# A decoder layer's first stage with its input scaling on ScalarE and low weight parts on VectorE, and its first query operands made during the value projections

## The chip, the cores and the metric

The kernel runs on one core of one Trainium2 chip. A core has five engines that run side by side, each from a queue of its own: TensorE (PE, with its weight loads, PEld), VectorE (DVE), ScalarE (ACT), GpSimd (POOL) and SyncE (SP), which here issues the DMAs. The metric is the device time of one execution in microseconds (us), the median of the runs shown.

## The reference

One layer for 1024 tokens of width 1024. What touches the change:

```python
mod = silu(c) @ w_mod + b_mod            # shift1, scale1, gate1, shift2, scale2, gate2
h   = x * (1.0 + scale1) + shift1
q, k, v, u, iq, ik, iw = split(h @ w_in) # 8 heads of 64; iq: 8 index heads of 64, ik: one
# rope on q, k, iq, ik
score = sum_h iw_h * relu(iq_h . ik)     # causal, one row per token
idx   = top_k(score, 256)                # per token
s = q . k / 8, only for keys in idx; softmax; o = p @ v
x = layer_norm(ALPHA * x + gate1 * (concat(o, pooled u) @ w_o))
x = layer_norm(ALPHA * x + gate2 * swiglu(x * (1 + scale2) + shift2))
```

## The kernel before

The 1024 tokens are eight tiles of 128. Matrices are kept as pairs of parts, a high part and a low part (the rest that rounding leaves), and a product is three passes of matmuls (high x high, high x low, low x high). `split(dst, raw, n, lo_eng)` makes such a pair of a weight block: the high part is a copy on ACT, the low part a subtraction on `lo_eng`, by default DVE (V). All instructions go through small queue objects, so each stands at one helper line (L174, DMAs L168) in the profile, and is told by its names.

Stages, with their times in the profiled execution:

1. **First stage, to 65 us.** Loop over the eight blocks j of 128 input channels (`for j in range(KT)`, L331): two dot products on DVE give scale and shift of the block (`mj`, in `const_C`); ACT makes hT's high part from the input `xt`; DVE scales `xt` in place (L350) and subtracts to get hT's low part; every second j the weights `WS[j // 2]` (`ws_W`) of the index query are split (L353), with the low part on DVE for j = 0 and on POOL for j = 2, 4, 6. Matmuls then add block j to the index queries of tiles 2 to 6 (`iq`) and to the index key (`ik`).
2. **Ropes and operands, to 87 us.** DVE ropes the index query of tile 2 and the index key (`ikt`, `ikr`); the weights of q (wq, four blocks into the same `ws_W`) are split at L457 to L463, low parts of blocks 0 and 2 on POOL, of 1 and 3 on DVE; POOL ropes tiles 3 to 7 (`iqraw`, `ptmp`); then the operands of the index scores (`ikE`, `ikO`, `qa`, `ql`). Projections `pj` fill PE in between.
3. **Index scores (lg), 87 to about 175 us**, tile by tile, with the q projections as filler. From then on the search for the 256 largest scores of each row runs as "streams": `bisect()` is a generator that yields before each piece of work with its engine and its length, and goes over bits of a 15-bit key, first of the high half of the score and then of the low half. There are four streams: tile 3, and tiles 5 and 4, whose rounds run on ACT (`keysA`, `junkB`, `colsA`); tile 2 (`LATE`; `keysA`, `colsE`, 128x384) and tiles 7 and 6 (`keysD`), whose rounds run on DVE. A planner models each queue's time; whenever an instruction would leave its engine idle for long enough, `fill()` puts the next piece of a stream ahead of it (`advance()`). LATE is not filled while tile 7 is being searched. `need(i)` runs the stream of tile i to its end at once.
4. **Projections, to 349 us**: 24 groups (`n_` = 0 to 23), eight of u, eight of k, eight of v, with `at_(n, f)` to put work behind group n. Then the operands of the queries of tiles 7 and 6 are made: `q_load` (DMA), `q_transpose` (PE, `qT`), `q_operands` (four ACT copies and two DVE subtractions each, `qab`).
5. **Attention, 365 to about 500 us**: 32 units of a tile and a head pair. A unit is `u_scores` (PE, `s`), masking by the searched scores with a row maximum on DVE (`sm_H`, `stat_X`), exponentials on ACT, transposes (`pT`) and the product with v (`pair`, `o`). Scores run two units ahead (`AHEAD`). Tiles 7 and 6 come first, then 5 and 4, 3 and 2, 1 and 0.
6. **Output projection, normalisation and the gated FFN (gu, dn), to 1291 us.**

While `pinned` holds an engine's letter, its instructions stay in the order in which the planner wrote them; elsewhere the scheduler may move them.

Of the kernel before, what the change touches and what calls it, by code (L numbers as in the profile page):

```python
# [186 lines left out]
def decoder_layer_kernel(  # L187
# [143 lines left out]
    for j in range(KT):  # L331
        wm = wmr[j % 3]
        for hf in range(2):
            SP.dma_start(wm[:, hf * 1024 : (hf + 1) * 1024], wma_in[j][:, hf * 1024 : (hf + 1) * 1024])
        xt = xtr[j % 7]
        SP.dma_start(xt, xT_in[j])
        if j == 0:
            SP.dma_start(bcol, bcol_in)
        if j % 2 == 0:
            raw_iq = raw_slot()  # L340
            SP.dma_start(raw_iq, wiq_in[j // 2])
        if j == 0:
            SP.dma_start(wik_raw, wikw_in)
        mj = m1[:, 2 * j : 2 * j + 2]
        for hf in range(2):
            dot(wm[:, hf * 1024 : (hf + 1) * 1024], mj[:, hf : hf + 1])
        V.tensor_tensor(mj, mj, bcol[:, 2 * j : 2 * j + 2], ALU.add)
        V.tensor_scalar(mj[:, 0:1], mj[:, 0:1], 1.0, None, ALU.add)
        A.activation(hT[j][:, 0:1024], xt, AF.Identity, bias=mj[:, 1:2], scale=mj[:, 0:1])
        V.tensor_scalar(xt, xt, mj[:, 0:1], mj[:, 1:2], ALU.mult, ALU.add)  # L350
        V.tensor_tensor(hT[j][:, 1024:2048], xt, f_(hT[j][:, 0:1024]), ALU.subtract)
        if j % 2 == 0:
            split(WS[j // 2], raw_iq, 1024, G if j else V)  # L353
        if j == 0:
            split(wik, wik_raw, 576)
        for t in range(2, 7):
            mm_k(psq[t], lambda k, a: hh(k, a, t * P, P), lambda k, b: ww(k, b, 0, 512), [j])
        for c in range(2):
            mm_k(psk[c][0:72, :], lambda k, b: wikk(k, b), lambda k, a: hh(k, a, c * 512, 512), [j])
# [95 lines left out]
                        float(np.float32(8.0 ** -0.5)), None, ALU.mult)  # L455
    rope_tok(V, iq_raw(2), iqtmp, 2)
    for kp in range(3):  # L457
        split(WS[kp], raws[kp], 1024, V if kp == 1 else G)
    raws[3] = raw_slot()
    SP.dma_start(raws[3], wq_in[3])  # L460
    for i in range(3, 7):
# [96 lines left out]
    biased = set()  # L558

    def bisect(tiles, cols, on_act):  # L560

# [9 lines left out]
        one = lambda c, m: c[:, m : m + 1]  # L571
        w_ = lambda i: (i + 1) / 8
        for m, i in enumerate(tiles):
            yield "V", 1.13 * w_(i)
            V.tensor_scalar(trash(i), score(i), 0.0, 0.0, ALU.is_ge, ALU.add, accum_out=one(cntc, m))
        yield "V", 0.6
        V.tensor_scalar(pr, cntc, float(TOPK), None, ALU.is_ge)
        V.tensor_scalar(sg, pr, 2.0, -1.0, ALU.mult, ALU.add)
        V.tensor_scalar(flip, pr, 32768.0, -32768.0, ALU.mult, ALU.add)
# [10 lines left out]
        sum_w = sum(w_(i) for i in tiles)  # L590

        def search_v(bits, base, low):
            V.memset(cand, float(1 << (bits - 1)))
            for b in range(bits - 1, -1, -1):
                yield "V", 0.4 + 1.08 * sum_w + 0.35 * nt
                for m, i in enumerate(tiles):
                    dt = U16 if low else I16
                    V.tensor_scalar(trash(i).bitcast(dt), kv[i].bitcast(dt), one(cand, m), one(base, m),
                                    ALU.is_ge, ALU.add, accum_out=one(cntc, m))
                off = -float(1 << (b - 1)) if b > 0 else -1.0  # L600
                for m in range(nt):
                    V.tensor_scalar(one(pr, m), one(cntc, m), 0.0, float(1 << b), ALU.is_ge, ALU.mult)
                for m in range(nt):
                    V.tensor_scalar(one(cand, m), one(pr, m), one(cand, m), off, ALU.add, ALU.add)

        def search_a(bits, low):

            V.memset(cand, 0.5 - float(1 << (bits - 1)))
            for b in range(bits - 1, -1, -1):
# [367 lines left out]
    qabh = buf("H", 14336, 1536, "qab", F32R)  # L977
    qabw = [buf("W", 2048 * i, 1536, "qab", F32R) for i in (0, 1)]
    qabx = [buf("X", 5312 + i * 1536, 1536, "qab", F32R) for i in (0, 1)]
    qab = {7: qabh, 6: qabw[0], 5: qabw[1], 4: qabw[0], 3: qabh, 2: qabx[0], 1: qabx[1], 0: qabh}  # L980

    qops = {}

    def q_load(i):
        raw = raw_slot()[:, 0:512]
        SP.dma_start(raw, q_d[i])
        return raw

    def q_make(i, raw, pt=None):
        b = qab[i]  # L990
        qops[i] = (b[:, 0:1024], b[:, 1024:1536])
        q_operands(pt if pt is not None else q_transpose(raw), *qops[i])

    for s_ in (last, last + 1):
        if s_ == last:
            qr = {i: q_load(i) for i in (7, 6)}
            qp = {i: q_transpose(qr[i]) for i in (7, 6)}
        for f in late.pop(s_, []):
            f()
    assert not late, late  # L1000
    for i in (7, 6):
        q_make(i, qr[i], qp[i])

    def cat_slot(g):
        return WS[g]

# [870 lines left out]
```

## Time and profile before

| | us |
|---|---|
| median of 3 runs | 1292.34 (1291.21 to 1293.01) |
| profiled execution | 1293.41, of which span 1291.6 |
| PE busy | 1200.3 (93%) |
| DVE busy | 994.8 (77%) |
| POOL busy | 722.5 (56%) |
| ACT busy | 654.5 (51%) |
| granted TensorE clock, mean | 0.972 of full |

The execution's own time is 1.8 us longer than the span of its instructions. A row of the waits reads: engine, its operation, the engine and the operation that it waited for, total time, how often, the longest. A row of instructions reads: start, duration, engine, line, operation, output and inputs, shapes, count; in brackets the idle time ahead of it and what ended that.

### The profile page before, as it was taken

Reading aid. Unit: us, or ns where it says so; the run is one execution under the profiler, and the core shown is the slowest. Engines: PE = TensorE matmul, PEld = TensorE weight load, DVE = VectorE, ACT = ScalarE, POOL = GpSimd, SP = SyncE. Lnnn points to the kernel's source line nnn. Section 1 sums busy time; section 2 is a strip of 40 time slices with the busy share of each in tenths; the row PEclk is TensorE's granted clock in tenths of the full one; section 3 lists DMA queues with packets and bytes.
Section 4 is the critical chain, followed back from the end, with each engine's and each line's share of the span. In section 5 each row is a group of like instructions: output and inputs, shape, how many; then the busy total and the mean of one; then the engine's idle time right before and its main releaser. Section 6 shows DMA issues by size and latency. Waiting matters only on the chain.

```text
span 1291.6 us, 16411 instructions
## 1 busy us (share of the span) xinstructions
PE 1200.3 (93%) x5622; PEld 932.2 (72%) x5622; DVE 994.8 (77%) x1845; ACT 654.5 (51%) x1343; POOL 722.5 (56%) x510
## 2 busy tenths in 40 slices
PE   7979999999879999997799999999999999999996
PEld 6656565687646666886678787878888787878775
DVE  6758998877979866568687778687877777687798
ACT  3346878797668687265443333343433333333531
POOL 1383375657012355267666657483847566576848
PEclk9989999999958999999899999999999999999998
DMA  9510048521000016300111021201121110203112
GB/s 350 200 72 17 10 159 321 196 82 57 17 1 17 9 50 214 129 9 9 65 66 66 33 82 34 82 33 66 33 65 39 60 66 33 90 33 107 49 66 114
DMA packets 32460, 103.40 MB, mean 80 GB/s; under 512 B 3573, under 2 KB 3573, under 8 KB 28793
## 3 DMA queue, kind: packets, MB, share of 16 engines
q1 hardware_dynamic: 32376, 102.36, 22.5%
q8 instruction: 44, 0.72, 0.2%
q14 instruction: 40, 0.32, 0.1%
HBM read 92.90 MB, written 9.45 MB: 79 GB/s over the span
## 4 chain that ended last, share of the span: by engine, by line
PE 60%; DVE 18%; POOL 9%; issue 7%; ACT 5%; DMA 1%; SPq 0%; DVEq 0%; POOLq 0%; ACTq 0%
PE gu L174 24%; PE dn L174 14%; PE pj L174 5%; PE wo L174 4%; PE pair L174 3%; PE s L174 2%; PE pT L174 2%; PE o L174 2%; DVE act_W L174 2%; DVE score_X L174 2%; POOL wraw_R L174 2%; DVE junk_X L174 2%; PE lg L174 2%; DVE utmp_X L174 1%; POOL ws_W L174 1%
## 5 line engine op out<-in xcount | busy, mean ns | idle before, releaser
L174 PE MATMUL gu<-hr_H,wblk_T 128*128 128x512 f32 (+1 forms) x924 | 217.5, 388 | 6.1 <-ACT gtmp_V L174 2.7
L174 PE MATMUL gu<-hr_H,wblk_V 128*128 128x512 f32 (+1 forms) x924 | 215.8, 385 | 4.3 <-POOL wblk_V L174 2.1
L174 PEld LDWEIGHTS gu<-hr_H,wblk_T 128*128 128x128 f32 x924 | 172.2, 191 | 42.4 <-POOL wblk_T L174 3.6
L174 PEld LDWEIGHTS gu<-hr_H,wblk_V 128*128 128x128 f32 x924 | 169.9, 188 | 41.4 <-POOL wblk_V L174 4.2
L174 DVE TENSOR_TENSOR res_X<-res_X,dn 128x512 f32<-128x512 f32 (+1 forms) x253 | 159.0, 679 | 15.4 <-PE dn L174 15.3
L174 PE MATMUL pj<-ws_W,hT_H 128*128 128x512 f32 x456 | 117.3, 406 | 8.8 <-POOL ws_W L174 6.7
L174 POOL TENSOR_TENSOR wraw_R<-wraw_R 128x512 f32<-128x512 f32 x64 | 94.6, 1486 | 47.0 <-DVE wblk_T L174 23.7
L174 POOL TENSOR_TENSOR wraw_W<-wraw_W 128x512 f32<-128x512 f32 x60 | 86.9, 1456 | 59.6 <-DVE wblk_V L174 29.3
L174 POOL TENSOR_SCALAR sm_H<-sm_H,stat_X 128x1024 f32<-128x1024 f32 (+7 forms) x64 | 48.0, 764 | 124.1 <-DVE stat_X L174 96.0
L174 PEld LDWEIGHTS pj<-ws_W,hT_H 128*128 128x128 f32 x456 | 85.0, 192 | 33.2 <-POOL ws_W L174 7.0
L174 PE MATMUL dn<-wblk_T,act_W 128*128 128x512 f32 x324 | 78.8, 391 | 4.3 <-DVE act_W L174 4.3
L174 PE MATMUL dn<-wblk_V,act_W 128*128 128x512 f32 x324 | 78.5, 391 | 2.9 <-DVE act_W L174 2.5
L174 DVE TENSOR_SCALAR_CACHE_REDUCE junk_X<-keysD_T,colsD_X 128x1024 int16<-128x1024 int16 (+1 forms) x64 | 78.9, 1268 | 0.2
L174 ACT ACTIVATE wblk_V<-wraw_R 128x512 fp32r<-128x512 f32 x56 | 35.2, 629 | 81.2 <-POOL wraw_R L174 62.7
L174 POOL TENSOR_TENSOR ws_W<-raw_R,ws_W 128x1024 fp32r<-128x1024 f32 x17 | 44.3, 2625 | 53.4 <-ACT ws_W L174 53.4
L174 PEld LDWEIGHTS dn<-wblk_T,act_W 128*128 128x128 f32 x324 | 60.4, 188 | 18.9 <-DVE act_W L174 6.4
L174 PEld LDWEIGHTS dn<-wblk_V,act_W 128*128 128x128 f32 x324 | 60.4, 188 | 17.4 <-DVE act_W L174 4.2
L174 ACT ACTIVATE wblk_V<-wraw_W 128x512 fp32r<-128x512 f32 x53 | 33.1, 627 | 75.0 <-POOL wraw_W L174 56.4
L174 ACT ACTIVATE wblk_T<-wraw_W 128x512 fp32r<-128x512 f32 x56 | 35.0, 628 | 65.9 <-POOL wraw_W L174 50.2
L174 ACT ACTIVATE wblk_T<-wraw_R 128x512 fp32r<-128x512 f32 x52 | 32.5, 627 | 60.5 <-POOL wraw_R L174 44.5
L174 ACT ACTIVATE utmp_X<-gu 128x512 f32<-128x512 f32 x33 | 19.7, 598 | 74.7 <-PE gu L174 74.7
L174 ACT ACTIVATE sm_H<-sm_H,stat_X 128x1024 f32<-128x1024 f32 (+7 forms) x64 | 49.1, 771 | 16.7 <-DVE stat_X L174 16.5
(295 smaller groups left out, 2763.7 us busy)
## 6 DMA issues: line engine op xcount, KB each, us to landing
mset_K<-in_wmr_dram SPq DMA_DIRECT2D x16, 1024.0 KB, 5.6
wm_K<-in_wma_dram SPq DMA_DIRECT2D x16, 512.0 KB, 10.0
wraw_R<-in_wg_dram SPq DMA_DIRECT2D x6, 1024.0 KB, 4.8
wraw_R<-in_wd_dram SPq DMA_DIRECT2D x12, 512.0 KB, 3.7
wraw_W<-in_wup_dram SPq DMA_DIRECT2D x12, 512.0 KB, 3.7
wraw_R<-in_wup_dram SPq DMA_DIRECT2D x10, 512.0 KB, 3.6
wraw_W<-in_wg_dram SPq DMA_DIRECT2D x5, 1024.0 KB, 4.9
wraw_W<-in_wd_dram SPq DMA_DIRECT2D x10, 512.0 KB, 3.5
```

The costliest lines, as they stand in the source:

```text
L174: ins_ = f(*a, **k)
```

## The change

In the first two stages the in-place scaling of `xt` becomes an ACT activation with the same scale and shift; the low parts of the index query's weights for j = 2, 4, 6 and of wq's blocks 0 and 2 go from POOL to DVE.

```diff
         A.activation(hT[j][:, 0:1024], xt, AF.Identity, bias=mj[:, 1:2], scale=mj[:, 0:1])
-        V.tensor_scalar(xt, xt, mj[:, 0:1], mj[:, 1:2], ALU.mult, ALU.add)
+        A.activation(xt, xt, AF.Identity, bias=mj[:, 1:2], scale=mj[:, 0:1])
         V.tensor_tensor(hT[j][:, 1024:2048], xt, f_(hT[j][:, 0:1024]), ALU.subtract)
         if j % 2 == 0:
-            split(WS[j // 2], raw_iq, 1024, G if j else V)
+            split(WS[j // 2], raw_iq, 1024)
         if j == 0:
             split(wik, wik_raw, 576)
...
     for kp in range(3):
-        split(WS[kp], raws[kp], 1024, V if kp == 1 else G)
+        split(WS[kp], raws[kp], 1024)
 
```

The rest is about the queries and searches. The operands of tiles 7 and 6 are made at groups 20 and 21, in buffers of their own (`qabv`, in V), from loads written at group 17; before, they are made behind the last group. From the last group on until the first two units are written, `hold` keeps `fill()` from placing any stream but the one of tiles 7 and 6 on DVE. DVE searches yield per tile and no longer per round of all their tiles. With every yield comes a flag that decides between streams that could start at the same time, and the pinning of a stream's first piece, which was LATE's alone, is given to every open stream behind the first two units.

```diff
             for b in range(bits - 1, -1, -1):
-                yield "V", 0.4 + 1.08 * sum_w + 0.35 * nt
                 for m, i in enumerate(tiles):
+                    yield "V", 0.3 + 1.08 * w_(i) + (0.35 * nt if m == nt - 1 else 0.0)
...
-        held = st[3] == LATE and st[4] and "V" not in pinned
+        held = st[4] and q.name not in pinned
...
-            todo = [st for st in streams if not (first and st[3] == LATE) and st[1][0] == q.name and start(st) + st[1][1] <= until + SLACK.get(q.name, 0.0)]
+            todo = [st for st in streams if not (first and st[3] == LATE) and not (hold and (q.name == "A" or 7 not in st[3])) and st[1][0] == q.name and start(st) + st[1][1] <= until + SLACK.get(q.name, 0.0)]
             if not todo:
                 return
-            advance(min(todo, key=lambda st: (start(st), st[3] not in TILES_A)))
+            advance(min(todo, key=lambda st: (start(st), not (len(st[1]) > 2 and st[1][2]))))
...
+    qabv = [buf("V", 4096 + 1536 * i, 1536, "qab", F32R) for i in (0, 1)]
+    qab = {7: qabv[0], 6: qabv[1], 5: qabw[1], 4: qabw[0], 3: qabh, 2: qabx[0], 1: qabx[1], 0: qabh}
...
+        if n_ == len(groups) - 1:
+            hold.append(1)
+        if n_ == 17:
+            qr.update((i, q_load(i)) for i in (7, 6))
+        if n_ in (20, 21):
+            at_(n_, lambda i=27 - n_: q_make(i, qr[i]))
...
     for s_ in (last, last + 1):
-        if s_ == last:
-            qr = {i: q_load(i) for i in (7, 6)}
-            qp = {i: q_transpose(qr[i]) for i in (7, 6)}
         for f in late.pop(s_, []):
             f()
     assert not late, late
-    for i in (7, 6):
-        q_make(i, qr[i], qp[i])
-
...
         u_exp(u)
+    hold.clear()
+    for st in streams:
+        st[4] = True
     u_norm(units[0])
```

What the engines' sequences of instructions show of it, at three places. A row is line, operation, output and inputs with their buffer numbers, and the output's shape.

POOL behind its constants, the first stage and the ropes, before (`ws_W` are low weight parts, `ptmp_C` and `iqraw_V` the ropes):

```order
L174 TENSOR_TENSOR ws_W_70<-raw_R_74,ws_W_70 128x1024
L174 TENSOR_TENSOR ws_W_71<-raw_R_75,ws_W_71 128x1024
L174 TENSOR_TENSOR ws_W_72<-raw_R_73,ws_W_72 128x1024
L174 TENSOR_TENSOR ws_W_69<-raw_R_74,ws_W_69 128x1024
L174 TENSOR_TENSOR ptmp_C_455<-iqraw_V_447,gr_G_76 128x512
```

and, behind three ropes and the first piece of the fourth, the last low part of wq among them:

```order
L174 TENSOR_TENSOR iqraw_V_447<-iqraw_V_447,ptmp_C_455 128x512
L174 TENSOR_TENSOR ptmp_C_455<-iqraw_V_447,gr_G_76 128x512
L174 TENSOR_TENSOR ws_W_71<-raw_R_73,ws_W_71 128x1024
L174 TENSOR_TENSOR iqraw_V_447<-iqraw_V_447,gr_G_76 128x512
L174 TENSOR_TENSOR iqraw_V_447<-iqraw_V_447,ptmp_C_455 128x512
```

and now:

```order
L174 MEMSET const_C_78 128x256
L174 AFFINE_SELECT const_C_78<-const_C_78 128x128
L174 TENSOR_TENSOR ptmp_C_455<-iqraw_V_447,gr_G_76 128x512
L174 TENSOR_TENSOR iqraw_V_447<-iqraw_V_447,gr_G_76 128x512
L174 TENSOR_TENSOR iqraw_V_447<-iqraw_V_447,ptmp_C_455 128x512
```

The ropes stand first on POOL now; no low weight part is left among or ahead of them.

DVE from the last block's low part of hT to the operands of the index scores, before (rows of the ropes between the first and the second piece are left out):

```order
L174 TENSOR_TENSOR const_C_78<-const_C_78 128x2
L174 TENSOR_SCALAR const_C_78<-const_C_78 128x1
L174 TENSOR_SCALAR xt_V_94<-xt_V_94,const_C_78 128x1024
L174 TENSOR_TENSOR hT_H_68<-xt_V_94,hT_H_68 128x1024
L174 TENSOR_TENSOR iqtmp_V_448<-iqraw_V_447,gr_G_76 128x512
```

```order
L174 TENSOR_SCALAR const_C_78<-ikt_477 128x32
L174 TENSOR_TENSOR ikr_X_499<-ikr_X_499,ikt_X_500 128x256
L174 TENSOR_TENSOR ws_W_70<-raw_R_75,ws_W_70 128x1024
L174 TENSOR_TENSOR ws_W_72<-raw_R_74,ws_W_72 128x1024
L174 TENSOR_TENSOR ikE_K_554<-ikT_563,ikE_K_554 64x512
```

and now:

```order
L174 TENSOR_TENSOR hT_H_68<-xt_V_94,hT_H_68 128x1024
L174 TENSOR_TENSOR ws_W_69<-raw_R_74,ws_W_69 128x1024
L174 TENSOR_TENSOR ws_W_70<-raw_R_75,ws_W_70 128x1024
L174 TENSOR_TENSOR iqtmp_V_448<-iqraw_V_447,gr_G_76 128x512
L174 TENSOR_TENSOR iqraw_V_447<-iqraw_V_447,gr_G_76 128x512
```

```order
L174 TENSOR_SCALAR const_C_78<-ikt_477 128x32
L174 TENSOR_TENSOR ikr_X_499<-ikr_X_499,ikt_X_500 128x256
L174 TENSOR_TENSOR ws_W_71<-raw_R_73,ws_W_71 128x1024
L174 TENSOR_TENSOR ws_W_72<-raw_R_74,ws_W_72 128x1024
L174 TENSOR_TENSOR ikE_K_554<-ikT_563,ikE_K_554 64x512
```

The scaling of `xt` is gone; two low parts of wq stand ahead of the rope of tile 2, two behind the ropes of the index key as before, so that the operands still follow a pair of low parts.

DVE around the first attention unit (`sm_H` from `s` is its masking, `junk_X` with `keysA_X` 128x384 a round of tile 2, `keys_T` and `junkA_T` the end of the search of tiles 5 and 4), before:

```order
L174 TENSOR_SCALAR colsE_X_610<-colsE_X_610 128x1 x2
L174 TENSOR_SCALAR junk_X_608,colsE_X_610<-keysA_X_599,colsE_X_610 128x384
L174 TENSOR_TENSOR qab_H_2672<-qT_2679,qab_H_2672 64x512 x2
L174 ISA sm_H_2671,stat_X_2666<-s_2757,score_X_77 128x1024
L174 ISA stat_X_2666 128x1
L174 TENSOR_TENSOR qab_W_2673<-qT_2684,qab_W_2673 64x512 x2
L174 ISA sm_H_2671,stat_X_2666<-s_2758,score_X_77 128x1024
```

and now:

```order
L174 TENSOR_SCALAR junkA_T_606,colsA_X_600<-score_X_77,colsA_X_600 128x640
L174 TENSOR_SCALAR colsA_X_600<-colsA_X_600 128x1
L174 TENSOR_SCALAR colsE_X_610<-colsE_X_610 128x1 x4
L174 TENSOR_TENSOR qab_V_1314<-qT_2660,qab_V_1314 64x512 x2
L174 ISA sm_H_2746,stat_X_2741<-s_2752,score_X_77 128x1024
L174 ISA stat_X_2741 128x1
```

and seven rows on:

```order
L174 RECIPROCAL stat_X_2741<-stat_X_2741 128x2
L174 ISA sm_H_2746,stat_X_2741<-s_2787,score_X_77 128x1024
L174 ISA stat_X_2741 128x1
L174 TENSOR_SCALAR score_X_77<-score_X_77 128x640
L174 TENSOR_TENSOR keysA_X_599<-score_X_77,colsE_X_610 128x384
L174 MEMSET colsE_X_610 128x1
L174 TENSOR_TENSOR keys_T_604<-keys_T_604,score_X_77 128x640
L174 TENSOR_SCALAR junk_X_608,colsE_X_610<-keysA_X_599,colsE_X_610 128x384
```

The rounds of tile 2 and the query operands stood ahead of the first masking; now one low part of tile 6 stands there, and the end of tile 4's search and the rounds of tile 2 come behind the maskings of the first two units. On ACT the copies of `qab_V` now stand among the last value copies, where `qab_H` and `qab_W` stood behind them. SP's queue of loads keeps its sequence.

More of the change, by code (lines that the diff above doesn't have):

```diff
@@ L556, in decoder_layer_kernel @@
     keys = {i: kw.bitcast(I16) for i, kw in keys.items()}
-    biased = set()
+    biased, hold = set(), []
     def bisect(tiles, cols, on_act):
@@ L573, in bisect @@
         for m, i in enumerate(tiles):
-            yield "V", 1.13 * w_(i)
+            yield "V", 1.13 * w_(i), on_act
             V.tensor_scalar(trash(i), score(i), 0.0, 0.0, ALU.is_ge, ALU.add, accum_out=one(cntc, m))
-        yield "V", 0.6
+        yield "V", 0.6, on_act
         V.tensor_scalar(pr, cntc, float(TOPK), None, ALU.is_ge)
@@ L583, in bisect @@
         for m, i in enumerate(tiles):
-            yield "V", 1.1 * w_(i)
+            yield "V", 1.1 * w_(i), on_act
             hv = score(i).bitcast(I16).rearrange("p (n two) -> p n two", two=2)
@@ L589, in bisect @@
                 V.tensor_scalar(one(thr, m), one(kp, m), 2.0, float(P * (i + 1) + 1), ALU.mult, ALU.add)
-        sum_w = sum(w_(i) for i in tiles)
         def search_v(bits, base, low):
@@ L619, in search_a @@
                     A.activation(one(cand, m), one(pr, m), AF.Identity, scale=-0.5 * float(1 << b), bias=one(cand, m))
-            yield "V", 0.1
+            yield "V", 0.1, True
             V.tensor_scalar(cand, cand, -1.0, None, ALU.mult)
@@ L625, in bisect @@
         for m, i in enumerate(tiles):
-            yield "V", 1.8 * w_(i)
+            yield "V", 1.8 * w_(i), on_act
             V.tensor_scalar(trash(i).bitcast(I16), kv[i], one(M, m), one(kp, m), ALU.is_gt, ALU.add,
@@ L666, in open_stream @@
         b = bisect(*a)
-        streams.insert(0, [T.t, next(b), b, a[0], True])
+        streams.insert(0, [T.t, next(b), b, a[0], a[0] == LATE])
         times.fill = fill
@@ L675, in advance @@
         q = queues[st[1][0]]
-        held = st[3] == LATE and st[4] and "V" not in pinned
+        held = st[4] and q.name not in pinned
         st[4] = False
         if held:
-            pinned.add("V")
+            pinned.add(q.name)
         try:
@@ L685, in advance @@
         if held:
-            pinned.discard("V")
+            pinned.discard(q.name)
         times.fill = fill
@@ L915, in take, with q_load, q_make @@
         at_(slot, lambda: k_transpose(t, raw))
+    qabh = buf("H", 14336, 1536, "qab", F32R)
+    qabw = [buf("W", 2048 * i, 1536, "qab", F32R) for i in (0, 1)]
+    qabx = [buf("X", 5312 + i * 1536, 1536, "qab", F32R) for i in (0, 1)]
+    qabv = [buf("V", 4096 + 1536 * i, 1536, "qab", F32R) for i in (0, 1)]
+    qab = {7: qabv[0], 6: qabv[1], 5: qabw[1], 4: qabw[0], 3: qabh, 2: qabx[0], 1: qabx[1], 0: qabh}
+    qops = {}
+    def q_load(i):
+        raw = raw_slot()[:, 0:512]
+        SP.dma_start(raw, q_d[i])
+        return raw
+    def q_make(i, raw, pt=None):
+        b = qab[i]
+        qops[i] = (b[:, 0:1024], b[:, 1024:1536])
+        q_operands(pt if pt is not None else q_transpose(raw), *qops[i])
     groups = [("u", g, c) for g in (3, 2, 1, 0) for c in range(2)] + [("k", t, 0) for t in range(NT)] + [("v", t, 0) for t in range(NT)]
@@ L920, in decoder_layer_kernel @@
     held, pair = {}, None
+    qr = {}
     for n_, (kind, a, b) in enumerate(groups):
+        if n_ == len(groups) - 1:
[4 more added lines that the diff above has]
+            at_(n_, lambda i=27 - n_: q_make(i, qr[i]))
         if n_ in PAIRS:
@@ L976, in decoder_layer_kernel @@
     smr = buf("H", 8192, 6144, "sm")
[L977 to L992, printed above, removed]
     for s_ in (last, last + 1):
-        if s_ == last:
-            qr = {i: q_load(i) for i in (7, 6)}
-            qp = {i: q_transpose(qr[i]) for i in (7, 6)}
         for f in late.pop(s_, []):
```

## The prediction

> **What bounds the kernel now.** I read the page's busy rows first, then TensorE's row by slices, then what TensorE waited for where that row dips, then those stretches in windows and instruction by instruction. The sum is made against the profiled execution, 1293.4 us with a span of 1291.6; the median of the three runs, 1292.3, lies 1.1 below it.
>
> ```profile
> PE 1200.3 (93%) x5622; PEld 932.2 (72%) x5622; DVE 994.8 (77%) x1845; ACT 654.5 (51%) x1343; POOL 722.5 (56%) x510
> PE   7979999999879999997799999999999999999996
> PEclk9989999999958999999899999999999999999998
> ```
>
> TensorE (PE) works 93% of the span. A slice is 32.3 us. What the change can reach is in the dips: slices 1 and 3 (up to 97 us), and slices 11 and 12 (323 to 387 us), of which the twelfth ran at about half the TensorE clock; the dips at 581 to 646 and at the end lie outside the change. Elsewhere PE is the limit, and a shorter time of another engine is worth nothing. What PE waited for, first up to 100 us, then from 280 to 520 us (total, times, longest):
>
> ```profile
> PE pj L174 <- POOL ws_W L174: 6.7, 1, 6.7
> PE iq L174 <- POOL ws_W L174: 3.7, 3, 1.4
> PE iq L174 <- DVE hT_H L174: 1.2, 2, 0.6
> ```
>
> ```profile
> PE s L174 <- ACT qab_H L174: 8.8, 1, 8.8
> PE s L174 <- DVE qab_H L174: 3.9, 1, 3.9
> ```
>
> Both edits aim at these rows: the low weight parts of stage one (ws_W) and the first query operands (qab_H). Windows say who is full there (PE, weight load, VectorE (DVE), ScalarE (ACT), POOL busy; then PE clock, DMA share, GB/s):
>
> ```profile
> 16.15:64.70 48.55, 43.63 (x177) 31.87 (x178) 40.32 (x59) 14.75 (x16) 13.94 (x5) 0.96 0.69 269
> 40.00:45.00 5.00, 3.64 (x16) 2.58 (x15) 4.93 (x8) 0.00 (x1) 2.35 (x1) 1.00 1.02 406
> 45.00:50.00 5.00, 5.00 (x23) 3.75 (x23) 4.42 (x8) 1.58 (x2) 0.00 (x0) 1.00 0.32 129
> 82.00:87.00 5.00, 4.86 (x11) 3.80 (x12) 0.00 (x0) 0.00 (x0) 4.76 (x5) 0.50 0.57 210
> 175.00:325.00 150.00, 144.99 (x689) 103.16 (x688) 122.72 (x298) 120.43 (x311) 96.57 (x60) 0.99 0.43 159
> 325.00:349.00 24.00, 24.00 (x112) 19.88 (x111) 23.84 (x57) 13.75 (x38) 0.00 (x0) 1.00 0.00 1
> 349.00:366.00 17.00, 4.31 (x13) 2.43 (x11) 15.39 (x52) 14.38 (x33) 0.00 (x0) 0.66 0.10 31
> 366.00:400.00 34.00, 31.64 (x140) 20.30 (x139) 27.05 (x80) 23.14 (x53) 10.65 (x10) 0.72 0.01 1
> 450.00:475.00 25.00, 24.75 (x170) 16.10 (x170) 15.84 (x45) 22.88 (x55) 13.33 (x14) 1.00 0.16 53
> ```
>
> From 16.15 us to the last ik matmul DVE is busy 40.32 of 48.55 us and ACT 14.75. Between 349 and 366 PE works 4.31 of 17 us while DVE and ACT are nearly full. From 175 to 349, and again from 450 on, PE is nearly full, so what is won before such a stretch is carried through it.
>
> **Stage one, part by part.**
>
> ```profile
> 14.87 1.22 DVE L174 TENSOR_TENSOR ws_W<-raw_R,ws_W 128x1024 fp32r<-128x1024 f32 x1
> 26.41 3.18 POOL L174 TENSOR_TENSOR ws_W<-raw_R,ws_W 128x1024 fp32r<-128x1024 f32 x1 [24.39 <-ACT ws_W L174]
> 27.28 3.39 DVE L174 TENSOR_TENSOR hT_H<-xt_V,hT_H 128x1024 fp32r<-128x1024 f32 x1
> 45.00 1.25 ACT L174 ACTIVATE hT_H<-xt_V,const_C 128x1024 fp32r<-128x1024 f32 x1 [5.90 <-DVE const_C L174]
> 46.28 0.81 DVE L174 TENSOR_SCALAR xt_V<-xt_V,const_C 128x1024 f32<-128x1024 f32 x1 [0.18 <-ACT hT_H L174]
> 59.88 1.23 DVE L174 TENSOR_TENSOR hT_H<-xt_V,hT_H 128x1024 fp32r<-128x1024 f32 x1
> 63.35 1.29 PE L174 MATMUL ik<-hT_H,wik_K 128*72 128x512 f32 x5
> 70.13 4.51 DVE L174 TENSOR_TENSOR ws_W<-raw_R,ws_W 128x1024 fp32r<-128x1024 f32 x2
> 76.08 0.69 DVE L174 TENSOR_TENSOR ikE_K<-ikT,ikE_K 64x512 fp32r<-64x512 f32 x1 [1.44 <-ACT ikO_K L174]
> 79.12 1.41 DVE L174 TENSOR_TENSOR ql_V<-qT,qa_K 64x512 fp32r<-64x512 f32 x2 [0.23 <-ACT qa_K L174]
> 82.14 5.06 PE L174 MATMUL pj<-ws_W,hT_H 128*128 128x512 f32 x11 [6.70 <-POOL ws_W L174]
> 87.00 0.52 PE L174 MATMUL lg<-ikE_K,qa_K 128*128 128x384 f32 x1
> ```
>
> DVE loses eight scalings of 0.81, 6.5. ACT takes them for 8 x 1.25 = 10 in 48.55 us of which it uses 14.75, so they are hidden, except that a tile's chain becomes 1.25 + 1.25 + 1.23. DVE takes three low parts of 1.22, 3.7. The subtraction of hT_H at 27.28 took 3.39 beside POOL's low part (26.41 to 29.59), the one at 59.88 only 1.23: three such collisions, gone, free up to 3 x 2.17 = 6.5. So DVE has 6.5 + 6.5 - 3.7 = 9.3 less to do, and the last low part of hT_H ends at about 52 where it ended at 61.1. It can hardly be earlier: at 40 to 45 us the DMA share is 1.02, at 45 to 50 it is 0.32 of 5, so inputs arrive until about 46.6 whatever DVE does, and the chain of 3.7 follows.
>
> PE then takes over as the limit: it has 43.63 us of work in the 48.55, and its idle there, 3.7 + 1.2 = 4.9, is all that can go. The last ik matmul ends at 59.7 instead of 64.64; of DVE's 9.3 no more than 4.9 shows.
>
> Behind it lies a chain on DVE: rope, wq low parts, low parts of the index keys, ql_V, then the first score matmul (lg, 87.00). The two low parts DVE had cost 4.51 while POOL worked beside them; it gets two more, of which two are done ahead of the rope, in the time that it now has over, and two stay behind. So that row only moves 4.9 earlier, from 70.13 to 65.2, and ends at 69.7. Four low parts of 0.69 and ql_V's 1.41 follow, with ACT's copies between them already under way: 73.9. Before the change PE's queue has eleven pj matmuls ahead of lg, and these wait 6.70 for POOL's last low part, issued behind three ropes and more; then they run at clock 0.50 (window 82 to 87), 5.06 us where half of that would do. With the low parts on DVE ahead of ql_V both are gone, and lg starts at about 73.5. **Gain D1 = 87.0 - 73.5 = 13.5.** The other way round it agrees: idle removed 4.9 + 6.7 = 11.6, half clock 2.5, together 14.1. Ends: 4.9 if lg is held by something else that moves only with PE; 15.6 if the 2.1 us by which POOL stretches the pair at 70.13 (4.51 against 2 x 1.22) go as well. I take 13.5, which the idle time of PE bears out. SP's queue of loads keeps its sequence; a load that waited for POOL to free its buffer now waits for DVE, which is sooner done.
>
> **Query operands and held searches.**
>
> ```profile
> 310.78 1.39 DVE L174 TENSOR_TENSOR kr_K<-kT,kr_K 64x512 fp32r<-64x512 f32 x2 [3.16 <-ACT kr_K L174]
> 344.94 1.55 DVE L174 TENSOR_TENSOR_SCAN score_X<-keys_T,colsA_X 128x640 bf16<-128x640 bf16 x1
> 348.49 1.03 PE L174 MATMUL qT<-const_C,raw_R 128*128 128x128 f32 x8
> 352.25 0.72 ACT L174 ACTIVATE junkB_X<-keysA_X,colsA_X 128x512 bf16<-128x512 uint16 x1
> 353.10 0.62 ACT L174 ACTIVATE colsA_X<-colsA_X 128x1 f32<-128x1 f32 x2
> 353.60 0.67 DVE L174 TENSOR_SCALAR_CACHE_REDUCE junk_X<-keysA_X,colsE_X 128x384 int16<-128x384 int16 x1
> 356.45 2.40 ACT L174 ACTIVATE qab_H<-qT 64x512 fp32r<-64x512 f32 x4
> 363.55 1.41 DVE L174 TENSOR_TENSOR qab_H<-qT,qab_H 64x512 fp32r<-64x512 f32 x2
> 365.54 1.22 DVE L174 CUSTOM_DVE_ANT_0 sm_H<-s,score_X 128x1024 f32<-128x1024 f32 x1 [0.59 <-PE s L174]
> 383.62 2.47 PE L174 MATMUL s<-kr_K,qab_H 128*128 128x512 f32 x8
> ```
>
> The operands of tiles 7 and 6 are made among the last v projections: ACT 2 x 2.40, DVE 2 x 1.41, PE 1.03, with their two loads at an unchanged place in SP's queue. ACT has cover there (13.75 of 24). DVE has none (23.84 of 24), but the finer filling lets the search of tiles 7 and 6 use waits such as the 3.16 at 310.78, about 2.5 rounds earlier by the sequences of instructions. So PE goes from the projections, with the qT matmuls now among them (349.52 in all), straight into eight s matmuls of 2.47 together: the first masked row (sm_H) starts at about 352.0 instead of 365.54, a lead of 13.5.
>
> The lead is not free. What stood in those 17 us now runs between the first attention units, on the same engines. DVE: nine rounds of tile 2 from 353.60 to 363.55, 9.95; their keys and the end of tile 4 (a scan of 1.55 and short steps), together some 3.9; less one 1.41 low part: 12.4. ACT: six more rounds of tiles 5 and 4, each 1.47 (352.25 to 353.72): 8.8. Against the DVE load stands its idle time from 366 to 400, 34 - 27.05 = 7.0; ACT has 10.9 idle there. If none of that can be used, 13.5 - 12.4 = 1.1 stays; if all, 8.1. I take the middle and round up, **D2 = 5**, because ACT's load alone fits. From 450 PE is full and carries it to the end. If the search returned nothing at all to the path, D2 would be 13.5.
>
> **Sum.** 13.5 + 5 = 18.5; 1293.4 - 18.5 = 1274.9, on the median's scale 1273.8.
>
> A row on the clock prices a hand-over that goes wrong. From 349 to 366 the mean clock is 0.66, and from 366 to 400 still 0.72 with PE busy 31.64 of 34: work alone did not bring full speed back. One such stretch costs about 0.28 x 31.64 = 8.9 us, and one more of it would make the sum 1273.8 + 8.9 = 1282.7. [...]
>
> **Rivals.**
> - The held searches give the whole second gain back (D2 at most 1): the units wait for the search rounds that DVE does between them. For: 12.4 us of search are 12.4 wherever they stand. Against: DVE's idle 7.0 up to 400. 1293.4 - 13.5 - 0.5 = 1279.4, on the median's scale 1278.3.
> - Slower: in the first attention units the clock does not come back. PE, waiting a little in each unit for DVE's search, stays at half clock as it did from 366 on. Each us of work at half costs another. It decides from 18.5 + 2.6 = 21 us of full-speed work done at half that ran at full before; at 30 us, about what PE works in such a stretch, the time would be 1273.8 + 30 = 1304. Against: the long idle stretch from 349, behind which the half clock stands, is what the change takes out.
> - The second gain is kept whole (D2 = 13.5), if search rounds fit into DVE's waits in all units up to 450: 1293.4 - 27 = 1266.4, on the median's scale 1265.3. For: PE alone sets the pace from 450. Against: DVE has 7.0 idle up to 400, not 12.4.
> - Stage one yields only PE's idle of 4.9, because lg waits for ACT's copies or POOL's ropes and not for low parts: 1293.4 - 4.9 - 5 = 1283.5, on the median's scale 1282.4. For: ikE_K at 76.08 waited 1.44 for ACT. Against: PE's 6.70 is on POOL's ws_W.
> - The change does nothing in effect, because DVE, with POOL's parts added, ends its chain when it did: 1292. The 9.3 us that it sheds speak against it.
>
> **Chances.** Forecast 0.48, its own range 1270 to 1278; search gives back 0.20; gain kept whole 0.12; stage one small 0.12; clock 0.06; nothing 0.02. The range from 1265 to 1284 takes in the first four, and so both ends of D1 and D2 singly. A difference under 0.2%, 2.6 us, can't be told from none here; by the cases faster 0.92, same 0.02, slower 0.06.
>
> **What the profile after would show.** In stage one: no POOL ws_W ahead of the index scores, no PE wait on POOL ws_W, last ik near 59.7, first lg near 73.5 at full clock. If lg starts after 80, D1 is wrong and the chain on DVE or POOL's ropes is what I misread. At the hand-over: no wait for qab_H, clock near 1.0, first sm_H 2 to 3 us behind the last v projection, rounds of tile 2 (128x384) among the first nine units. If PE's waits for stat_X or for ACT in those units add up to over 10 us, the search gave the gain back; if TensorE's clock stands at 0.5 over more than 20 us there, the slow rival holds.

## The result, and the profile after

The changed kernel takes 1270.07 us (median of 4 runs, 1267.85 to 1272.18) against 1292.67 for the kernel before in the same comparison: a ratio of 0.9826 with a 95% interval of 0.9806 to 0.9845, or 22.5 us (20.0 to 25.1). Forecast were 1274 and a range of 1265 to 1284. The profiled execution took 1269.91 us, its span 1268.1. One run of the experiment without the hold (2332 us) and one of that with wq's low parts on POOL (5905 us) were far off and are left out of the ratios below.

From the page of the changed kernel, engines' busy time, then TensorE (PE) and its granted clock in 40 slices of 31.7 us:

```profile
PE 1197.6 (94%) x5622; PEld 930.9 (73%) x5622; DVE 998.7 (79%) x1842; ACT 662.4 (52%) x1351; POOL 709.3 (56%) x505
PE   7999999999998999996899999999999999999996
PEclk8999999999897999998999999999999999999998
```

PE's dip of slice 3 and the one at the hand-over to attention (slices 11 and 12 before) are gone; PE's busy time is nearly the same in a span shorter by 23.5 us. The clock still dips: where it stood at 0.5 and 0.8 in slices 12 and 13, it stands at 0.8 and 0.7 in slices 11 and 13. What PE waited for in the changed kernel, up to 100 us and then from 280 to 520 us (total, times, longest):

```profile
PE iq L174 <- ACT ws_W L174: 4.9, 1, 4.9
PE pj L174 <- DVE const_C L174: 0.8, 1, 0.8
PE iq L174 <- DVE ws_W L174: 0.7, 1, 0.7
PE pj L174 <- DVE ws_W L174: 0.6, 1, 0.6
```

```profile
PE s L174 <- DVE stat_X L174: 4.2, 6, 1.4
PE s L174 <- DVE qab_W L174: 4.0, 1, 4.0
```

Up to 100 us no wait for POOL's low parts is left, and from 280 us on none for the first operands. The wait for a first high part from ACT has grown from 2.6 to 4.9 us, and there is a new one of 4.0 us for a later operand (`qab_W`); both are spoken of below. Rows of the changed kernel at the stage boundaries:

```profile
53.66 1.23 DVE L174 TENSOR_TENSOR hT_H<-xt_V,hT_H 128x1024 fp32r<-128x1024 f32 x1 [2.59 <-ACT xt_V L174]
54.81 2.35 DVE L174 TENSOR_TENSOR ws_W<-raw_R,ws_W 128x1024 fp32r<-128x1024 f32 x2
59.61 1.07 PE L174 MATMUL ik<-hT_H,wik_K 128*72 128x512 f32 x4
66.19 4.54 DVE L174 TENSOR_TENSOR ws_W<-raw_R,ws_W 128x1024 fp32r<-128x1024 f32 x2
72.05 0.34 PE L174 MATMUL lg<-ikE_K,qa_K 128*128 128x384 f32 x1
73.49 1.40 DVE L174 TENSOR_TENSOR ql_V<-qT,qa_K 64x512 fp32r<-64x512 f32 x2
323.07 11.18 PE L174 MATMUL pj<-ws_W,hT_H 128*128 128x512 f32 x48
335.85 1.23 DVE L174 CUSTOM_DVE_ANT_0 sm_H<-s,score_X 128x1024 f32<-128x1024 f32 x1 [3.50 <-PE s L174]
419.15 0.94 DVE L174 CUSTOM_DVE_ANT_0 sm_H<-s,score_X 128x768 f32<-128x768 f32 x1
491.42 8.32 PE L174 MATMUL wo<-hr_H,ws_W 128*128 128x512 f32 x36
```

The first lg moved from 87.00 to 72.05 us, 14.95 earlier. The last v projection ends at 334.25 and not at 348.65, 14.40 earlier with the qT matmuls now ahead of it. The first masking (sm_H) starts at 335.85 and not at 365.54, 29.69 earlier, so the lead of attention over the projections grew by 15.3. At unit 12 the masking starts at 419.15 instead of 441.09: 21.94 earlier, so 7.5 of the 15.3 are left. The output projection (`wo` from `hr_H`) keeps that: 491.42 against 514.13, 22.71.

Where the other 7.8 went, windows show: from the end of the last v projection to unit 12, and the 150 us ahead of it (columns as before: PE, weight load, VectorE (DVE), ScalarE (ACT), POOL busy; PE clock, DMA share, GB/s). The kernel before:

```profile
348.65:441.09 92.44, 73.06 (x389) 48.25 (x386) 82.43 (x253) 68.10 (x151) 22.21 (x22) 0.82 0.04 12
198.65:348.65 150.00, 146.81 (x695) 109.23 (x695) 123.66 (x303) 118.01 (x305) 78.87 (x49) 0.99 0.35 129
```

The changed kernel:

```profile
334.25:419.15 84.90, 75.13 (x384) 48.51 (x383) 75.02 (x236) 63.11 (x148) 22.91 (x22) 0.84 0.03 7
184.25:334.25 150.00, 147.04 (x700) 109.73 (x699) 130.93 (x310) 121.70 (x307) 78.61 (x49) 0.99 0.37 131
```

The stretch is 7.5 us shorter, DVE has 7.4 us less to do in it (82.43 to 75.02), and DVE's idle time is the same, 10.0 and 9.9. The 150 us ahead hold 7.3 us more DVE work. So the stretch is shorter by the work that DVE had done before it began. That DVE sets the pace here is so far read from the two equal idle times; the experiments test it.

### The profile page after: what moved, and what is told of

Same layout as the page of the kernel before. It is cut to its first block, busy times and chain, and to the rows that moved or that the text cites. A ratio compares the mean times of both kernels' runs of the same rounds, so it can differ in the third digit from the quotient of the medians.

```text
span 1268.1 us, 16420 instructions
## 1 busy us (share of the span) xinstructions
PE 1197.6 (94%) x5622; PEld 930.9 (73%) x5622; DVE 998.7 (79%) x1842; ACT 662.4 (52%) x1351; POOL 709.3 (56%) x505
## 4 chain that ended last, share of the span: by engine, by line
PE 67%; DVE 14%; POOL 6%; ACT 6%; issue 5%; DMA 1%; SPq 0%; DVEq 0%; POOLq 0%; ACTq 0%
PE gu L174 25%; PE dn L174 15%; PE pj L174 7%; PE wo L174 4%; PE pair L174 3%; PE pT L174 3%; PE s L174 2%; PE iq L174 2%; DVE act_W L174 2%; PE o L174 2%; POOL wraw_R L174 2%; PE lg L174 1%; DVE stat_C L174 1%; DVE utmp_X L174 1%; DVE junk_X L174 1%
## 5 line engine op out<-in xcount | busy, mean ns | idle before, releaser
L174 DVE TENSOR_TENSOR res_X<-res_X,dn 128x512 f32<-128x512 f32 (+1 forms) x253 | 158.9, 677 | 15.4 <-PE dn L174 15.3
L174 DVE SCALAR_TENSOR_TENSOR score_X<-relu_K,const_C,score_X 128x384 f32<-128x384 f32 (+5 forms) x42 | 54.2, 1290 | 5.0 <-ACT relu_K L174 1.4
L174 ACT ACTIVATE junkA_T<-keys_T,colsA_X 128x768 bf16<-128x768 uint16 (+3 forms) x62 | 54.4, 877 | 3.8 <-DVE colsA_X L174 2.9
```

The source lines that it names most:

```text
L174: ins_ = f(*a, **k)
```

## The experiments

All times are medians, and the ratios are to the kernel before on the same chip; gains are worked out from the ratio, times 1293 us. Two kernels first that each hold one half of the change.

**One half each.** Stage one only is the kernel before with the three edits of its first two stages:

```diff
-        V.tensor_scalar(xt, xt, mj[:, 0:1], mj[:, 1:2], ALU.mult, ALU.add)
+        A.activation(xt, xt, AF.Identity, bias=mj[:, 1:2], scale=mj[:, 0:1])
-            split(WS[j // 2], raw_iq, 1024, G if j else V)
+            split(WS[j // 2], raw_iq, 1024)
-        split(WS[kp], raws[kp], 1024, V if kp == 1 else G)
+        split(WS[kp], raws[kp], 1024)
```

> The scaling on ScalarE and all low weight parts on VectorE, with queries and searches as before. Theory (the two halves of the change add, and PE carries stage one's 15.0 us, the shift of the first lg, to the end): 1292.5 - 15 = 1277.5, between 1275.5 and 1279.5, first lg near 72. Rival (what stage one wins is lost again in the wait ahead of attention, because the searches there don't get earlier): the first masking moves by less than 10 us and the time stays above 1283.

The other kernel is the change with these three lines put back.

> Stage one as before; early query operands, hold, finer yields and pins as in the change. Theory (the halves add; the lead at the first masking is 14.4 us, of which about 7.5 is left after unit 10): 1292.5 - 7.5 = 1285, between 1283 and 1287. Rival (the searches need the earlier start that stage one gives them, so that alone the held searches give all back): 1290 or more.

Stage one alone: 1280.94 us, ratio 0.9899 (0.9885 to 0.9913), 13.1 us. Its first lg is at 72.32. Queries and searches alone: 1282.93 us, ratio 0.9922 (0.9910 to 0.9934), 10.1 us. Together 23.2, where the change has 22.5: the halves add, and both rivals fall. Both times lie outside the spans that I had given, the first above and the second below, by 1.4 us and less: the first half was put too high by some 2 us, the second too low by 2.6.

**The scaling alone.** The change with the scaling of `xt` on DVE again (the first two lines of the diff reversed).

> The whole change, but the scaling of xt on VectorE again (eight times 0.81 us). Theory (VectorE has 9.9 us idle in the first loop, 43.85 - 33.96, so 6.5 more fit; the low parts are what counted): first lg before 74 and within 2 us of 1270. Rival (the scaling stands in the chain of the last blocks, and the last low part of hT comes later by it): first lg after 75 and 1274 to 1276.

1267.80 us, ratio 0.9806 (0.9790 to 0.9822); the first lg at 71.52, 0.5 earlier than in the change. The scaling on ACT gains nothing. Whether it costs the 2 us between the medians can't be told, as the intervals overlap. The window from 16.15 to 60 us, in this kernel and then in the changed one:

```profile
16.15:60.00 43.85, 42.97 (x179) 32.51 (x180) 38.27 (x64) 14.82 (x14) 0.00 (x0) 0.96 0.82 316
```

```profile
16.15:60.00 43.85, 43.39 (x180) 33.41 (x181) 33.96 (x57) 23.05 (x22) 0.15 (x1) 0.94 0.81 316
```

With the scaling DVE is busy 38.27 of 43.85 us and still has room; PE is full either way.

**The low parts of iq.** The change with `G if j else V` in the first loop again.

> The whole change, but the low parts of the index query's weights for j = 2, 4, 6 on GpSimd again. Theory (of stage one's 15.0 us wq's low parts were worth 4.5, so 10 lie in the first loop, most of it here: PE waits 3.7 us for these parts, they stretch VectorE's subtractions from 1.2 to 3.4 us and keep GpSimd from the ropes): first lg at 76 to 80 and 1274 to 1278. Rival (the scaling was worth most of it): first lg before 74.5 and within 2 us of 1270.

1274.94 us, ratio 0.9862 (0.9845 to 0.9878), 4.6 us less gain than the change. The first lg is at 77.83, inside the span. Two rows of this kernel say how:

```profile
61.85 1.07 PE L174 MATMUL ik<-hT_H,wik_K 128*72 128x512 f32 x4
68.45 6.73 DVE L174 TENSOR_TENSOR ws_W<-raw_R,ws_W 128x1024 fp32r<-128x1024 f32 x3
```

The index key ends 2.2 us later than in the change, and DVE then has three of wq's low parts behind its ropes, at 2.2 us each beside POOL's ropes (the low part at 59.32 in this kernel, ahead of POOL's first rope at 62.09, took 1.22), where the change has two (66.19, 4.54): the other was done in DVE's free time ahead of the rope.

**The low parts of wq.** The change with `V if kp == 1 else G` again.

> The whole change, but the low parts of wq's blocks 0 and 2 on GpSimd again, behind and among the ropes. Theory (stage one's 15.0 us are 4.9 us of idle in the first loop plus 10 us of the wait for that low part and of half clock behind it): the first lg at 80 to 83 and 1278 to 1281. Rival (GpSimd, which has no low parts of iq any more, reaches the ropes and wq early enough): first lg before 76 and at most 1274.

1274.59 us, ratio 0.9855 (0.9835 to 0.9874), 3.8 us less gain; the first lg at 76.55. That lies between theory and rival, and the theory's 10 us for this part is wrong. POOL and PE in this kernel:

```profile
PE pj L174 <- POOL ws_W L174: 3.1, 1, 3.1
```

```profile
60.20 1.31 POOL L174 TENSOR_TENSOR ptmp_C<-iqraw_V,gr_G 128x512 f32<-128x512 f32 x1 [2.84 <-ACT iqraw_V L174]
69.94 2.34 POOL L174 TENSOR_TENSOR ws_W<-raw_R,ws_W 128x1024 fp32r<-128x1024 f32 x1
76.55 0.34 PE L174 MATMUL lg<-ikE_K,qa_K 128*128 128x384 f32 x1
```

Without iq's low parts POOL starts its ropes at 60.20 (63.63 before the change) and gets to wq's last low part at 69.94 (79.75 before), so PE waits 3.1 us for it and no longer 6.7. The interval still overlaps that of the change, and that of the kernel with iq's low parts on POOL touches it, so the shifts of the first lg are the firmer figures. Of the 15.0 us at lg, giving back wq alone costs 4.5 and iq alone 5.8. That makes 10.3. The other 4.7 show only when both are on POOL, where the low parts of iq hold up the ropes and, behind them, wq's last low part.

**The hold.** The change without `hold.append(1)`.

> The whole change without the hold: the searches of tiles 2, 5, 4 and 3 may again be filled ahead of the first attention unit; in the sequence eight rounds of tile 2 then stand ahead of the first masking. Theory (search work costs the same wherever it stands, as VectorE is nearly full until unit 10): the first masking comes some 9 us later, but the block of eight rounds that now stands at unit 9 is shorter, and the time is within 3 us of 1270. Rival (the hold is what earns the second gain): 1276 to 1279.

1271.25 us, ratio 0.9835 (0.9819 to 0.9851): the same as the change. The first masking starts at 344.87, 9.0 later than with the hold; unit 10 starts at 408.38 (408.46 with it). The stretch in this kernel:

```profile
334.28:419.40 85.12, 70.87 (x384) 44.59 (x383) 74.68 (x237) 61.26 (x136) 23.77 (x22) 0.84 0.03 7
```

85.12 us with 74.68 of DVE work, 84.90 with 75.02 in the change. The hold moves search work from ahead of the first unit to behind it; the sum of it stays.

**The operands.** The change with operands loaded, transposed and made behind the last projection, as before it.

> The whole change, but the operands of tiles 7 and 6 are loaded, transposed and made behind the last projection as before, with hold and finer yields left in. Theory (VectorE's work sets the pace: only the 2.8 us of low parts come back into the stretch, and VectorE's idle time while ScalarE copies, about 5 us, since hold forbids filling it): 1276 to 1279. Rival (work is conserved and the idle time is made up for in the units): 1271 to 1274.

1276.59 us, ratio 0.9870 (0.9855 to 0.9884), 5.7 us less gain. The time lies in the theory's span, but not by the theory's way. The 150 us up to the end of the projections (332.73 us), the stretch from there to unit 12, and unit 12 to 17, in this kernel:

```profile
182.73:332.73 150.00, 146.80 (x708) 108.73 (x705) 122.67 (x285) 116.88 (x299) 81.20 (x50) 1.00 0.37 135
332.73:419.75 87.02, 76.08 (x388) 48.54 (x386) 79.42 (x231) 69.40 (x163) 23.13 (x22) 0.84 0.05 13
419.75:449.95 30.20, 28.39 (x174) 18.72 (x173) 23.76 (x77) 21.57 (x49) 12.12 (x13) 0.90 0.09 27
```

And unit 12 to 17 in the changed kernel:

```profile
419.15:443.12 23.97, 23.80 (x169) 16.09 (x169) 16.38 (x44) 20.50 (x46) 11.67 (x13) 1.00 0.09 34
```

Unit 12 starts at 419.75, only 0.6 us later than in the change, and DVE's idle time in the stretch did not grow by 5 us: it is 7.6, and 9.9 in the change. The loss comes behind unit 12, where 30.20 us pass and not 23.97. DVE did 8.3 us less ahead of the stretch (122.67 against 130.93) and has 7.4 us more to do behind it (23.76 against 16.38), and the mean clock there is 0.90 and not 1.00. How much of the 6.2 us is due to which of the two is open.

**The size of the pieces.** The change with a yield per round.

```diff
-                for m, i in enumerate(tiles):
-                    yield "V", 0.3 + 1.08 * w_(i) + (0.35 * nt if m == nt - 1 else 0.0)
+                yield "V", 0.4 + 1.08 * sum(w_(i) for i in tiles) + 0.35 * nt
+                for m, i in enumerate(tiles):
```

> The whole change, but VectorE's searches yield once per round again, not once per tile of a round. Theory (from the last value projection to unit 12 VectorE's work sets the pace; the change shortened the stretch because finer pieces let 7.4 us of that work be done in gaps of the projections before it): VectorE's work in that stretch grows by 4 to 7.4 us and the time is 1274 to 1278. Rival (the early operands alone are the gain, the size of the pieces does nothing): within 2 us of 1270.

1272.10 us, ratio 0.9841 (0.9826 to 0.9855), 2.0 above the change and not to be told from it, as the intervals overlap. The theory's 1274 to 1278 is missed. The 150 us ahead of the end of the projections, the stretch to unit 12, and unit 12 to 17, in this kernel:

```profile
185.15:335.15 150.00, 146.78 (x698) 109.29 (x698) 121.85 (x292) 121.14 (x305) 78.04 (x48) 0.99 0.36 130
335.15:418.93 83.78, 72.62 (x384) 46.65 (x383) 75.16 (x222) 62.66 (x148) 23.99 (x22) 0.88 0.03 7
418.93:445.41 26.48, 24.73 (x170) 16.69 (x171) 23.17 (x74) 20.82 (x47) 11.29 (x12) 1.00 0.10 31
```

The finer pieces do get 9.1 us more of DVE's work done ahead (130.93 against 121.85). But the stretch did not grow, since rounds of tile 2 went behind unit 12 instead, where DVE has 23.17 us of work and 16.38 in the change. Work can be moved out of the stretch at either end. Put back one at a time, the late operands cost 5.7 us, the coarse pieces 2.0 and the missing hold 1.2, and only the first is clear of the intervals.

**DVE's work as the pace.** Two tries to take work out. First, of the transposed probabilities' copies in tiles 7 to 4 none is made by DVE:

```diff
-                if n_cp[0] % COPY_N in COPY_V:
+                if g < 2 and n_cp[0] % COPY_N in COPY_V:
```

> The whole change, and in the units of tiles 7 to 4 the one copy of transposed probabilities in four that VectorE makes (0.56 to 0.68 us each) goes to ScalarE, where the other three are. Theory (VectorE's work sets the pace up to unit 12): twelve copies less, about 7 us, and 1263 to 1266. Rival (ScalarE, or TensorE at its lower clock, is right behind VectorE): within 2 us of 1270, or slower.

1278.34 us, ratio 0.9890 (0.9876 to 0.9905): 8 us slower than the change, and the theory falls in this form.

```profile
334.12:426.81 92.69, 73.71 (x383) 47.48 (x383) 75.14 (x230) 66.24 (x157) 23.36 (x22) 0.82 0.02 7
```

DVE's work did not shrink: 75.14 where the change has 75.02. In the sequence two blocks of nine rounds of tile 2 now stand among the units, and DVE's idle time rose from 9.9 to 17.6 us. So it is no test of less work. The blocks are the likely cause of the idle time, but no run here takes them alone out of this kernel. ACT got the copies and is not fuller for it: it has 26.5 us idle here (92.69 less 66.24) and 21.8 in the change.

Second, tile 2's rounds themselves are moved. One kernel keeps each of its pieces where the planner wrote it (in the change only the first):

```diff
-        st[4] = False
+        st[4] = st[3] == LATE
```

> The whole change, with every piece of tile 2's search kept at the place where the planner wrote it, not its first piece alone; in the sequence the block of eight rounds ahead of the low parts of a query operand (PE's wait of 3.97 us there) becomes one of five. Theory (that block costs PE 3 to 5 us, which no later stretch gives back): 1266 to 1268. Rival (VectorE's total up to unit 17 decides, not where a block stands): within 1.5 us of 1270.

1269.18 us, ratio 0.9816 (0.9803 to 0.9829): not to be told from the change, where the theory had asked for 1266 to 1268. What it was aimed at, in the changed kernel, rows of DVE, of ACT and of PE:

```profile
388.38 0.65 DVE L174 TENSOR_SCALAR_CACHE_REDUCE junk_X<-keysA_X,colsE_X 128x384 uint16<-128x384 uint16 x1
396.44 0.67 DVE L174 TENSOR_SCALAR_CACHE_REDUCE junk_X<-keysA_X,colsE_X 128x384 uint16<-128x384 uint16 x1
397.04 1.40 DVE L174 TENSOR_TENSOR qab_W<-qT,qab_W 64x512 fp32r<-64x512 f32 x2
```

```profile
391.57 0.59 ACT L174 ACTIVATE qab_W<-qT 64x512 fp32r<-64x512 f32 x1
```

```profile
397.77 0.90 PE L174 MATMUL s<-kr_K,qab_W 64*128 64x512 f32 x2 [3.97 <-DVE qab_W L174]
```

Eight rounds stand in a row from 388.38; ACT's part of the operand is done at 392.16, DVE gets to its low part at 397.04, and PE waits 3.97 us. Breaking the block up makes unit 9 1.7 us earlier and unit 12 3.3 us, but the time hardly at all. The stretch to unit 12 in this kernel:

```profile
334.26:415.82 81.56, 72.11 (x381) 46.80 (x379) 73.59 (x221) 62.01 (x146) 22.50 (x22) 0.85 0.03 7
```

The others keep that edit and add a pace: at unit n no more than 6 + 3n, or 4 + 2.2n, pieces of tile 2 may have been filled. The lines that count the pieces are left out here.

```diff
+    def quota():
+        return 6 + 3.0 * un[0]
-            todo = [st for st in streams if not (first and st[3] == LATE) ...
+            todo = [st for st in streams if not (st[3] == LATE and (first or late_n[0] >= quota())) ...
```

> The whole change, with tile 2's search kept in the planner's order and paced: at unit n at most 6 + 3n of its pieces may have been filled, so that about 8 of its rounds stand behind unit 12's masking (one in the change). Tile 2 is needed from unit 17 on. Theory (VectorE's work sets the pace up to unit 12, and behind it VectorE has idle time): 1262 to 1267. Rival (VectorE's total up to unit 17 is what counts, or TensorE at its lower clock is right behind): 1268 to 1272.

> As the kernel paced with 6 + 3n, but with 4 + 2.2n pieces: some 15 rounds of tile 2, 16.6 us, stand behind unit 12's masking. Theory (VectorE has about 9 us idle between units 12 and 17, so half of that load only shifts the wait there): no better than the faster pace, 1264 to 1269. Rival (only the stretch up to unit 12 is bound by VectorE): 1256 to 1260.

1266.61 us, ratio 0.9793 (0.9776 to 0.9809), and 1266.50 us, ratio 0.9796 (0.9781 to 0.9810). Both are the fastest here by median, 3.5 us below the change; but the intervals still touch that of the change (from 0.9806), and a better kernel is not shown. To unit 12 and to unit 17, first with 6 + 3n, then with 4 + 2.2n, then the change:

```profile
334.85:414.25 79.40, 70.59 (x380) 44.78 (x379) 67.83 (x197) 61.69 (x146) 22.56 (x22) 0.89 0.03 8
334.85:440.63 105.78, 95.51 (x552) 61.79 (x552) 91.50 (x278) 83.22 (x194) 33.73 (x34) 0.92 0.05 13
```

```profile
334.26:411.55 77.29, 68.53 (x384) 43.29 (x383) 61.63 (x174) 61.99 (x148) 22.74 (x22) 0.93 0.03 8
334.26:441.40 107.14, 95.71 (x568) 61.07 (x567) 90.61 (x275) 85.37 (x198) 34.75 (x35) 0.95 0.05 13
```

```profile
334.25:443.12 108.87, 98.92 (x552) 64.61 (x552) 91.40 (x277) 83.61 (x194) 34.59 (x35) 0.87 0.04 13
```

Only the pace sets these two apart from the kernel that keeps the order, which has 73.59 us of DVE work in 81.56 us. Against that, taking 5.8 us of work out (67.83) shortens the way to unit 12 by 2.2 us, and 6.2 more (61.63) by 2.1. So below some 74 us of work DVE no longer sets the pace by itself; what does, no run here shows.

For that DVE sets it above, the windows of all fourteen kernels speak. In eleven of them, the kernel before and the change among them, DVE's idle time in the stretch lies between 7.6 and 10.4 us, with 73.6 to 82.4 us of work. The other three are the two paced ones (11.6 and 15.7) and the one with the blocks (17.6).

Up to unit 17, for which tile 2 must be done, DVE's work is 91 us in the two paced kernels and in the change: what was put off comes due there. Against the change they were 5.5 and 7.6 us ahead on the way to unit 12, and 3.1 and 1.7 us of that are left.

## Why the prediction was right, and where it was not

The direction, the time within 4 us, and both places were right: 13.5 + 5 forecast, 22.5 measured, 14.4 + 7.5 = 21.9 in the traces at unit 12. The terms were off in these steps.

- **Scalings, 6.5 us off DVE:** freed as said, and worth nothing. DVE had room for them, as the reversed edit shows.
- **PE's idle of 4.9 goes, last ik at 59.7:** it ended at 60.68. The idle was gone (43.39 of 43.85), but PE started 0.5 us later, behind a first high part on ACT. It waited 4.9 us for that, 2.6 before the change; the wait is 2.4 to 3.0 in the three kernels with the scaling on DVE and 3.4 to 5.1 in those with it on ACT. This price of ACT's longer queue I had left out.
- **Chain on DVE, lg at 73.5:** 72.05. The steps that I listed add up to 73.9, and to 72.5 without ql_V. The pair of wq's low parts ran at 66.19 (65.2 forecast), but the first lg does not need ql_V, which I had put ahead of it; it started 1.4 us before ql_V. So D1 is 15.0 at lg and 13.1 measured by itself, with 13.5 forecast.
- **The 6.7 wait goes because wq leaves POOL:** only in part. More than half of that wait came from iq's low parts ahead of the ropes. The sum held since both moved.
- **The rival that stage one yields only 4.9, and the upper end of D1:** the rival fell. D1 reached 15.0 of its upper end 15.6, but not for the reason given there: the pair of low parts still took 4.54 us beside POOL's ropes, where the pair at 54.81, with POOL idle, took 2.35.
- **Lead of 13.5 at the first masking:** 15.3. PE went from the projections into the first scores (334.08) without a wait and at full clock (1.00 from 334 to 337 us), as said; the masking started 1.6 us behind the last v projection, where 2 to 3 were forecast.
- **D2 = 5, the term that was mis-sized:** I had 12.4 us of search come back and DVE's idle 7.0 take up half of it. In fact the idle time up to unit 12 took up none of it (10.0 and 9.9 us), while the work that came back was less: DVE does 7.3 us more ahead of the end of the projections. That takes the finer pieces and the earlier operands together; with either one put back it does 121.85 and 122.67 us there, where the change does 130.93 and the kernel before 123.66. Two errors offset each other in part, which is luck; D2 was 7.5 in the change and 10.1 by itself. I should have compared DVE's sum of work over the stretch, and not the length of what is moved with idle time of one window.
- **The clock and the slow rival:** I had expected a clock near 1.0 at the hand-over. Its mean over the stretch to unit 12 is 0.84, hardly above the 0.82 before. An estimate from these means, with the clock taken as either 1.00 or 0.50, puts some 27 us of the stretch at half clock, against some 33 before. Over the whole stretch that is more than the 20 us that I had named as the sign of the slow rival, and yet the rival did not come: the kernel before had no less, which the sign left out. What half clock costs here can be read from a pair of runs once, about 1 us for some 9 us of it; see below.

## What to carry to other kernels

Where one engine sets the pace of a stretch and its idle time does not change, a reordering is worth the work that is done before the stretch begins: add up that engine's work between two fixed points, before and after. Work that is put off behind the end of the stretch comes due there, so a second point further on has to be looked at too. Two pieces of work on the same helper engine need not add up: putting back either alone cost 4.5 and 5.8 us at the first lg, while the change, which moves both, won 15.0. Taking the scaling, 6.5 us of work, off an engine that had room gained nothing.

## What the runs showed of the hardware

The granted clock differs between executions of the same sequence: over the four runs of the changed kernel its mean was 0.977, 0.982, 0.977 and 0.977. In the changed kernel and in the one with the scaling on DVE, PE waits the same 1.41 us between its first groups of attention scores, and the order of instructions from there on is the same, engine by engine. The changed kernel, rows of five windows:

```profile
337.00:340.00 3.00, 2.77 (x8) 1.39 (x8) 2.32 (x6) 2.73 (x5) 0.00 (x0) 0.79 0.00 0
340.00:343.00 3.00, 3.00 (x6) 1.46 (x6) 2.65 (x5) 2.31 (x5) 0.00 (x0) 0.50 0.02 5
343.00:346.00 3.00, 3.00 (x10) 1.70 (x10) 3.00 (x6) 1.76 (x6) 2.66 (x2) 0.50 0.00 0
346.00:349.00 3.00, 3.00 (x14) 2.64 (x12) 3.00 (x11) 2.69 (x6) 0.00 (x0) 0.50 0.00 0
349.00:352.00 3.00, 3.00 (x17) 1.96 (x17) 3.00 (x8) 2.31 (x6) 2.65 (x3) 1.00 0.00 0
```

The kernel with the scaling on DVE, two such windows and the stretch to unit 12:

```profile
336.00:339.00 3.00, 2.43 (x8) 1.19 (x8) 2.67 (x6) 2.38 (x4) 0.00 (x0) 1.00 0.00 0
339.00:342.00 3.00, 2.74 (x9) 1.18 (x8) 2.93 (x5) 2.93 (x6) 0.13 (x1) 1.00 0.02 5
333.59:417.47 83.88, 71.36 (x385) 45.63 (x383) 75.05 (x235) 62.90 (x148) 22.92 (x22) 0.90 0.02 7
```

In the one the clock falls to 0.50 for some 9 us in which PE's row is full, in the other it stays at 1.00. From the first masking to unit 12 they take 83.30 and 82.28 us, so this piece of half clock goes with 1.0 us. DVE's work in the stretch is the same, 75.02 and 75.05 us, and fits the reading that DVE sets the pace there. Later pieces of lower clock stand in both kernels (0.67 from 380 to 390 us and 0.65 from 400 to 410 in the changed one; a mean of 0.90 over the stretch in the other, with 1.00 up to 351 us), and what they cost is not shown. Full speed came back within PE's full rows, after about 9 us of them in the changed kernel. In the kernel before PE's row was full from 370 to 386 us, with a mean clock of 0.50 up to 378 and of 0.76 from there; the prediction had read from the mean of 0.72 that work alone did not bring full speed back. What does, no run here shows.
